# A hybrid decoder step: one more pipeline step between the root of a chunk's norm and the matrix that spreads it

## The chip, the cores and the metric

The kernel runs on one core of a Trainium2 chip. The metric is the device time of one execution in microseconds. Three executions of the kernel before took 1460.03, 1463.79 and 1465.53 us; the median is 1463.79 us.

## The reference

One layer of a decoder for 528 prompt tokens (16 learned ones and 512 given) and 64 sample tokens, with two branches side by side: a Mamba-2 state space branch and an attention branch over keys that an indexer chooses; sigmoid gates merge them, and a squared-ReLU MLP follows. The change lies in the state space branch, of which this matters:

```
# per chunk of 128 tokens, per group of 8 heads (4 groups of 512 channels)
y = einsum(cc·bc, decay, x*dt) + einsum(cc, h) * exp(acum)     # within the chunk, and from the state h
h = h * exp(last) + einsum(wj, x*dt, bc)                       # the next chunk's state
y = (y + x * d_skip) * silu(z)
y = y * rsqrt(mean(y*y over the group's 512 channels) + eps) * ssm_norm_w
```

Here tokens stand in columns and channels in partitions, so the mean over channels goes across partitions.

## The kernel before, in words

Projections, attention and MLP are matrix products in which an fp32 number is split into a rounded part and a rest (`split`, L121), so that each product is three matmuls (`mm3`, L140, issued at L145). Their weights come by DMA into a raw tile `wr`; ScalarE rounds them to `wh` (L122), VectorE makes the rest `wl` (L123).

The state space stage weaves three sources of work together. `conv_tile` and `z_tile` compute 24 + 16 tiles of the input projection (L145). `states` handles the samples' states, four units to a group. `chunk` handles one chunk of one group; there are 4 groups with 5 chunks each, in the order c = 4 (the 64 sample tokens), 0, 1, 2, 3. Each is a generator; `Pipe.push` (L91) takes in one more unit and lets every live unit run to its next `yield`, the oldest first. A group takes nine pushes: four units of `states`, then five chunks. `scan.run()` (L826) pushes on until nothing is live.

`chunk` has four steps before the change:

- the loads of `sz`, `xd`, `EB` and `bc`, the decay exponentials (L729, L731), and the product B·C with its mask (L734, L736);
- eight scaled decay tiles (L741) and their matmuls (L742), the product with the carried state (L754), the sum `y1` of both parts (L759, L760), the next state (L765 to L768), then y with skip and gate (L770, L771), its squares (L773) and their sums over the four blocks of 128 channels (L774, L775);
- a matmul with ones that sums over partitions and puts tokens in partitions (L779), and `rstd_of` (L781): mean and eps on VectorE (L154), the power -0.5 on GpSimd (L155), giving one number `ss` per token; then `rd`, a diagonal matrix with those numbers (L783, VectorE);
- a matmul of `rd` with ones that spreads the numbers over all partitions (L786, "the spread"), the scaling of `y1` by them and the norm's weight (L788, four instructions), and the write of `y1` to DRAM, `d_y` (L790). For c = 3 the final state is transposed and written too (L792 to L798).

Buffers: `y1` has three, allocated at L757 in the second step and free once the write of L790 has read it (`ho`, L796, takes one too); `ss`, `rd`, `sz`, `xd` and `EB` have two. PSUM tiles come from three tags: "w" (2 banks, projections), "a" and "s" (3 each).

What Python issues is not yet the order on an engine: the framework's scheduler places the instructions, by data dependences, free buffers and the order of issue, and so one `yield` shifts other work too. On each engine the order is then fixed. All DMAs of this stage but the gathers go through SyncE's queue, in order. The sixteen gate tiles (`gate`, L555) and the first part of the sample attention (`sample`, L849, with gathers into `Kg` and `Vg`, L860) follow, and are drawn in wherever engines have room.

Of the kernel before, what the change touches and what calls it, by code (L numbers as in the profile page):

```python
# [70 lines left out]
def body(ctx, tc, a, o):  # L71
# [42 lines left out]
    def K(n):  # L114
        s, e = CONSTS[n]
        return cst[0][:, s:e] if e <= KEPT else cst[1][:, s - KEPT:e - KEPT]
# [36 lines left out]
    def rstd_of(dst, ssq, n, cols, p=128):  # L153
        dve.tensor_scalar(dst, ssq, 1.0 / n, EPS, op0=OP.mult, op1=OP.add)  # L154
        pool.tensor_tensor(dst, dst, K("half")[:p, :cols], op=OP.pow)  # L155
# [475 lines left out]
    with tc.tile_pool(name="p3", bufs=1, reuse_waits="tile") as p3, \  # L631
# [78 lines left out]
        def chunk(g, c):  # L710
# [68 lines left out]
            pe.matmul(ps[:n, 0:1], sq[:, 0, :n], K("ones")[:, 0:1], start=True, stop=True)  # L779
            ss = p3.tile([128, 1], FT, tag="ss", name="ss", bufs=2)  # L780
            rstd_of(ss[:n], ps[:n, 0:1], 512, 1, n)  # L781
            rd = p3.tile([128, 128], FT, tag="rd", name="rd", bufs=2)
            dve.tensor_scalar(rd[:n, :n], idf[:n, :n], ss[:n], None, op0=OP.mult)  # L783
            yield
# [31 lines left out]
        for g in range(4):  # L816
            start(g)
            for j in range(9):
                scan.push(states(g, j) if j < 4 else chunk(g, (4, 0, 1, 2, 3)[j - 4]))
                next(tops, None)  # L820
                for _ in range(1 if j else 2):
                    if nxt:
                        conv.push(nxt.pop(0))
            if not nxt:
                conv.run()
# [603 lines left out]
```

## Time and profile before

| | |
|---|---|
| profiled execution, its own time | 1456.66 us |
| its span (first to last instruction) | 1454.9 us |
| median of three executions | 1463.79 us |
| TensorE (PE) matmul | 1417.8 us busy, 97% |
| VectorE (DVE) | 1096.0 us, 75% |
| ScalarE (ACT) | 755.6 us, 52% |
| GpSimd (POOL) | 328.7 us, 23% |

The chunks of the state space stage run from about 310 to 665 us of the span. Times in the rows below are in us from the span's start unless marked ns; L123 is line 123 of the kernel; "out<-in" are the program's tile names; "[x <-E t Ln]" tells how long the engine sat idle before the instruction and what ended that.

### The profile page before, as it was taken

The numbers are of one execution on the slowest core, as the hardware profiler recorded it, in microseconds if no ns is written. First come the engines' busy times: TensorE is split into PE (matmuls) and PEld (weight loads), VectorE is DVE, ScalarE is ACT, GpSimd is POOL, SyncE is SP. The second block draws the span as 40 slices with busy tenths as digits, with TensorE's granted clock in tenths as the row PEclk, the third lists the DMA queues.
The fourth block names the chain that finished last, engine by engine and source line by source line (L and its number), as shares of the span: only waits on it lengthen the run. The fifth ranks groups of instructions, "written<-read, shape, count | busy, mean of one in ns | idle before, by whom it ended". The sixth has DMA issues, their size and how long they took to land.

```text
span 1454.9 us, 26523 instructions
## 1 busy us (share of the span) xinstructions
PE 1417.8 (97%) x9808; PEld 1270.7 (87%) x9808; DVE 1096.0 (75%) x2248; ACT 755.6 (52%) x1719; POOL 328.7 (23%) x479
## 2 busy tenths in 40 slices
PE   8999999999999998999999999999999999999998
PEld 6998999988898987989688988898798988888986
DVE  6799999898769778482645777765689887888775
ACT  5553365556566655443655777832374554445441
POOL 2110011436446436251433633100000000000001
PEclk9999999999999999999999999999999999999999
DMA  7334464567676767768974532235233322322222
GB/s 204 88 76 123 126 162 126 140 194 216 181 223 184 209 185 213 222 180 260 295 240 132 154 88 85 69 104 178 80 90 100 92 89 81 88 92 86 88 70 73
DMA packets 258907, 206.73 MB, mean 142 GB/s; under 512 B 38653, under 2 KB 225905, under 8 KB 258754
## 3 DMA queue, kind: packets, MB, share of 16 engines
q1 hardware_dynamic: 253530, 186.16, 45.1%
q0 software_dynamic: 5248, 18.88, 3.9%
q8 instruction: 77, 1.26, 0.4%
q14 instruction: 52, 0.43, 0.1%
HBM read 167.83 MB, written 36.40 MB: 140 GB/s over the span
## 4 chain that ended last, share of the span: by engine, by line
PE 50%; DVE 1%; DMA 1%; issue 0%; ACT 0%; POOL 0%; POOLq 0%; DVEq 0%; ACTq 0%; SPq 0%
PE s L1184 15%; PE w L1049 7%; PE a L1309 6%; PE w L145 5%; PE w L1309 4%; PE a L145 3%; PE s L1015 2%; PE s L881 2%; PE a L1184 1%; PE a L1005 1%; PE a L904 1%; PE s L873 1%; PE s L984 1%; PE s L983 1%; PE a L894 1%; DMA jk<-h 0%
## 5 line engine op out<-in xcount | busy, mean ns | idle before, releaser
L145 PE MATMUL w<-uh,wh 128*128 128x288 f32 (+1 forms) x1168 | 359.7, 308 | 9.8 <-ACT qis L348 2.9
L145 PE MATMUL w<-ul,wh 128*128 128x288 f32 (+1 forms) x1168 | 353.5, 303 | 1.2 <-DVE ul L225 1.2
L145 PE MATMUL w<-uh,wl 128*128 128x288 f32 (+1 forms) x1168 | 354.6, 304 | 0.0
L145 PEld LDWEIGHTS w<-uh,wh 128*128 128x128 f32 x1168 | 223.9, 192 | 17.8 <-issue 4.2
L145 PEld LDWEIGHTS w<-ul,wh 128*128 128x128 f32 x1168 | 223.8, 192 | 4.4 <-issue 2.2
L145 PEld LDWEIGHTS w<-uh,wl 128*128 128x128 f32 x1168 | 222.7, 191 | 2.1 <-issue 1.7
L123 DVE TENSOR_TENSOR wl<-wr,wh 128x1024 fp32r<-128x1024 f32 x129 | 159.5, 1237 | 75.6 <-ACT wh L122 74.8
L122 ACT ACTIVATE wh<-wr 128x1024 fp32r<-128x1024 f32 x129 | 135.7, 1056 | 137.6 <-PE w L145 76.6
L1186 DVE TENSOR_TENSOR h<-h,s 128x512 f32<-128x512 f32 (+1 forms) x161 | 108.4, 680 | 57.7 <-PE s L1184 57.4
L1184 PE MATMUL s<-dh,hh 128*128 128x512 f32 (+1 forms) x302 | 118.8, 393 | 0.0
L1184 PE MATMUL s<-dl,hh 128*128 128x512 f32 (+1 forms) x302 | 118.7, 393 | 0.0
L155 POOL TENSOR_TENSOR rs<-rs,cst 128x1 f32<-128x1 f32 (+2 forms) x15 | 9.3, 619 | 415.1 <-DVE rs L154 415.0
L1184 PE MATMUL s<-dh,hl 128*128 128x512 f32 (+1 forms) x242 | 95.0, 392 | 0.0
L1049 PE MATMUL w<-ysh,wh 128*128 128x288 f32 x256 | 78.3, 308 | 0.2 <-DVE ms L1054 0.2
L122 ACT ACTIVATE dh<-wr 128x1024 fp32r<-128x1024 f32 x38 | 39.8, 1057 | 72.7 <-PE s L1184 58.5
L1049 PE MATMUL w<-ysh,wl 128*128 128x288 f32 x256 | 76.7, 300 | 0.0
L1049 PE MATMUL w<-ysl,wh 128*128 128x288 f32 x256 | 76.7, 300 | 0.0
L729 ACT ACTIVATE bc<-bc,acum 128x128 f32<-128x128 f32 (+1 forms) x160 | 49.2, 379 | 49.3 <-DMA bc<-d_ac 40.6
L594 DVE SCALAR_TENSOR_TENSOR ca<-rb,cwT,ca 128x616 f32<-128x616 f32 x72 | 68.8, 956 | 1.8 <-ACT ca L592 1.2
L1184 PEld LDWEIGHTS s<-dl,hh 128*128 128x128 f32 x302 | 56.6, 188 | 12.5
L1184 PEld LDWEIGHTS s<-dh,hh 128*128 128x128 f32 x302 | 56.7, 188 | 10.0 <-DVE h L1186 0.2
L741 DVE SCALAR_TENSOR_TENSOR bc<-bc,dts,cb 128x128 f32<-128x128 f32 (+1 forms) x160 | 57.5, 426 | 0.3
(499 smaller groups left out, 3689.9 us busy)
## 6 DMA issues: line engine op xcount, KB each, us to landing
wr<-in_w_in_dram SPq DMA_DIRECT2D x64, 512.0 KB
wr<-in_w_up_dram SPq DMA_DIRECT2D x32, 512.0 KB
wr<-in_w_down_dram SPq DMA_DIRECT2D x32, 512.0 KB
st<-in_state_ssm_dram SPq DMA_DIRECT2D x16, 512.0 KB
bc<-d_ac SPq DMA_DIRECT2D x32, 256.0 KB
out_dram<-st SPq DMA_DIRECT2D x16, 512.0 KB
wr<-in_w_ssm_proj_dram SPq DMA_DIRECT2D x16, 512.0 KB
EB<-d_ec SPq DMA_DIRECT2D x40, 128.0 KB
```

Source lines behind the costliest of these rows:

```text
L122: act.activation(hi, raw, AF.Copy)
L123: (lo_eng or dve).tensor_tensor(lo, raw, hi.bitcast(FT), op=OP.subtract)
L145: pe.matmul(ps[:, :c1 - c0], p[:, k, :], x[:, c0:c1], start=(k == 0 and i == 0), stop=(k == 7 and i == 2))
L594: dve.scalar_tensor_tensor(ca[:, 0:616], rb[:, k:k + 616], cwT[:, 24 * k + ct:24 * k + ct + 1], ca[:, 0:616], op0=OP.mult, op1=OP.add)
L729: act.activation(bc[:n, i, :n], bc[:n, i, :n], AF.Relu, scale=-1.0, bias=acum[:n, c, h0 + i:h0 + i + 1])
L741: dve.scalar_tensor_tensor(mt, mt, dts[:n, c, 8 * g + hh:8 * g + hh + 1], cb[:n, :n], op0=OP.mult, op1=OP.mult)
L881: pe.matmul(v[64 * hp:64 * hp + 64], QZ[:, hp, :], kk, start=True, stop=True)
L1015: pe.matmul(py[64 * e:64 * e + 64, 0:256], Vt[:, j, kv:kv + 64], PT[:, e, j], start=(j == 0), stop=False)
L1049: pe.matmul(ps[:, :HQ], p[:, k, mc], x[k][:, c0:c1], start=(k == 0 and i == 0), stop=(k == 3 and i == 2))
L1184: pe.matmul(ps, p, w[:, cc], start=(k == 0 and i == 0), stop=(k == len(ws) - 1 and i == len(terms) - 1))
L1186: dve.tensor_tensor(h2[:, t, cc], h2[:, t, cc], ps, op=OP.add)
L1309: pe.matmul(ps, p[:, k, :], q[:, k, :], start=(k == 0 and j == 0), stop=(k == 3 and j == 2))
```

## The change

One `yield` is put into `chunk`, after `rstd_of` and ahead of `rd`. What was the third step becomes two: the sum and the root stay at the push where they were, `rd` is issued one push later, and the spread, the scaling, the write to DRAM and (for c = 3) the final state's transposes and write one push later than before.

```
             ss = p3.tile([128, 1], FT, tag="ss", name="ss", bufs=2)
             rstd_of(ss[:n], ps[:n, 0:1], 512, 1, n)
+            yield
             rd = p3.tile([128, 128], FT, tag="rd", name="rd", bufs=2)
             dve.tensor_scalar(rd[:n, :n], idf[:n, :n], ss[:n], None, op0=OP.mult)
             yield
             rr = pst("a")
```

Lines from L782 on are one higher in the kernel after: `rd` is L784, the spread L787, the scaling L789, the write L791. No instruction is added or removed on any engine; orders differ from the second chunk on, on into the attention stages.

TensorE around chunk c = 2 of the third group, before: from that chunk's sum (L779) to its spread (L786) with what stands between (34 rows of L145 are left out).

```order
L779 MATMUL a<-cst,xd 128x1
L685 MATMUL a<-cst,st 128x128 x8
L145 MATMUL w<-uh,wh 128x288
...
L145 MATMUL w<-uh,wl 128x288
L786 MATMUL a<-rd,cst 128x128
L145 MATMUL w<-uh,wh 128x288
```

After: the first L787 here is that of the chunk before (c = 1), the second that of c = 2.

```order
L779 MATMUL a<-cst,xd 128x1
L685 MATMUL a<-cst,st 128x128 x8
...
L787 MATMUL a<-rd,cst 128x128
...
L699 MATMUL s<-Bz,xr 128x512 x3
...
L779 MATMUL a<-cst,xd 128x1
L693 MATMUL a<-sT,BC 32x128 x8
L685 MATMUL a<-cst,st 128x128 x4
...
L787 MATMUL a<-rd,cst 128x128
```

The spread of c = 2 stood 45 TensorE instructions behind its sum and stands 127 behind it now, behind the sum of c = 3.

VectorE at the end of the same group, before: `y1_6725` is c = 0's, `y1_7022` is c = 3's, which takes the same buffer, three allocations later.

```order
L788 SCALAR_TENSOR_TENSOR y1_6725<-y1_6725,nwT_84,a_6841 128x128 x4
L154 TENSOR_SCALAR ss_6850<-a_6848 128x1
...
L771 TENSOR_TENSOR y1_6877<-y1_6877,sz_6816 128x512
L788 SCALAR_TENSOR_TENSOR y1_6801<-y1_6801,nwT_84,a_6986 128x128 x4
L759 TENSOR_TENSOR y1_7022<-s_7017,EB_6894 128x512
```

After, the same two chunks are `y1_6723` and `y1_7013`.

```order
L789 SCALAR_TENSOR_TENSOR y1_6723<-y1_6723,nwT_84,a_6977 128x128 x4
L768 TENSOR_TENSOR hn_7020<-hn_7020,s_7018 128x512
L154 TENSOR_SCALAR ss_6988<-a_6986 128x1
L759 TENSOR_TENSOR y1_7013<-s_7008,EB_6885 128x512
L760 TENSOR_TENSOR y1_7013<-y1_7013,s_6991 128x512
L784 TENSOR_SCALAR rd_7051<-cst_66,ss_6988 128x128
L123 TENSOR_TENSOR wl_7901<-wr_7900,wh_7902 128x1024
```

Between the last use of the buffer by the older chunk and the first write of it by the newer stood ten rows, and stand two now; the DMA that reads the buffer has to end between them. The same pairs, of chunks c = 2 and c = 3, stand closer in the other groups too.

## Rows read from the trace of the kernel before

**Rows 1.** The page: span, busy time of PE, ACT and others.
```profile
span 1454.9 us, 26523 instructions
PE 1417.8 (97%) x9808; PEld 1270.7 (87%) x9808; DVE 1096.0 (75%) x2248; ACT 755.6 (52%) x1719; POOL 328.7 (23%) x479
```
**Rows 2.** Windows, the moved stretch: window, PE, PEld, DVE, ACT, POOL busy, clock, DMA.
```profile
290.00:700.00 410.00, 396.67 (x3048) 355.20 (x3046) 297.98 (x568) 221.84 (x537) 178.48 (x205) 0.99 0.73 207
```
**Rows 3.** Waits of PE, 290 to 700 us: total us, times, longest.
```profile
PE a L786 <- DVE rd L783: 3.1, 1, 3.1
PE w L145 <- ACT tg L283: 2.6, 2, 1.9
PE a L625 <- ACT sT L686: 2.2, 1, 2.2
...
PE s L742 <- DVE bc L741: 1.2, 3, 0.7
...
PE a L779 <- POOL xd L775: 0.8, 2, 0.4
```
**Rows 4.** Timeline of PE at the longest wait: start, duration, instruction.
```profile
575.45 0.29 PE L145 MATMUL w<-ul,wh 128*128 128x288 f32 x1
575.58 0.29 PE L145 MATMUL w<-uh,wl 128*128 128x288 f32 x1
578.93 0.49 PE L786 MATMUL a<-rd,cst 128*128 128x128 f32 x2 [3.06 <-DVE rd L783]
```
**Rows 5.** Timeline of DVE just before it.
```profile
576.96 1.92 DVE L783 TENSOR_SCALAR rd<-cst,ss 128x128 f32<-128x128 f32 x1
```
**Rows 6.** Timeline of POOL just before it.
```profile
576.45 2.34 POOL L687 TENSOR_TENSOR st<-st,elc 128x1024 f32<-128x1024 f32 x1
```
**Rows 7.** All instructions of L783: ns min/median/max, first and last start.
```profile
L783 DVE TENSOR_SCALAR rd<-cst,ss x20: 239/284/1923, 338.3 to 658.9; 128x128 f32<-128x128 f32 x16, 64x64 f32<-64x64 f32 x4
```
**Rows 8.** Windows behind two waits of PE, and one in between at full clock.
```profile
579.50:582.90 3.40, 3.40 (x18) 3.40 (x17) 2.40 (x6) 3.40 (x8) 1.33 (x1) 0.56 0.23 60
586.30:589.70 3.40, 3.40 (x37) 3.17 (x26) 0.28 (x1) 1.37 (x3) 0.55 (x1) 1.00 1.03 288
392.30:395.50 3.20, 3.20 (x14) 3.01 (x14) 2.65 (x7) 3.08 (x8) 0.25 (x2) 0.50 0.83 239
```
**Rows 9.** Timeline of SP (DMA issues), two places.
```profile
351.23 0.45 SPq L727 DMA_DIRECT2D bc<-d_ac  x1
...
663.79 0.46 SPq L790 DMA_DIRECT2D d_y<-y  x1
```
**Rows 10.** Who waited for the landing: ACT for bc, POOL for d_y.
```profile
354.08 1.06 ACT L729 ACTIVATE bc<-bc,acum 64x64 f32<-64x64 f32 x4 [0.83 <-DMA bc<-d_ac]
...
670.45 0.94 POOL L860 DMA_INDIRECT Vg<-in_cache_v_dram,idx  x1 [2.78 <-DMA d_y<-y]
```
**Rows 11.** Waits of SP's queue, 290 to 700 us.
```profile
SPq L790 <- DVE y L788: 13.2, 5, 4.8
```
**Rows 12.** Groups of DVE: busy us, mean ns of one, idle before.
```profile
L123 DVE TENSOR_TENSOR wl<-wr,wh 128x1024 fp32r<-128x1024 f32 x129 | 159.5, 1237 | 75.6 <-ACT wh L122 74.8
...
L594 DVE SCALAR_TENSOR_TENSOR ca<-rb,cwT,ca 128x616 f32<-128x616 f32 x72 | 68.8, 956 | 1.8 <-ACT ca L592 1.2
L741 DVE SCALAR_TENSOR_TENSOR bc<-bc,dts,cb 128x128 f32<-128x128 f32 (+1 forms) x160 | 57.5, 426 | 0.3
...
L768 DVE TENSOR_TENSOR hn<-hn,s 128x512 f32<-128x512 f32 x16 | 10.9, 680 | 0.9 <-PE s L765 0.8
```
**Rows 13.** Timeline of POOL: the sum of squares of c = 2, groups 1 and 2.
```profile
364.51 0.50 POOL L775 TENSOR_TENSOR xd<-xd 128x128 f32<-128x128 f32 x1
...
473.54 0.46 POOL L775 TENSOR_TENSOR xd<-xd 128x128 f32<-128x128 f32 x1
```
**Rows 14.** Timeline of PE: the matmuls that take these sums.
```profile
366.91 0.28 PE L779 MATMUL a<-cst,xd 128*128 128x1 f32 x2
...
474.05 0.38 PE L779 MATMUL a<-cst,xd 128*128 128x1 f32 x2 [0.35 <-POOL xd L775]
```

More of the change, by code (lines that the diff above doesn't have):

```diff
@@ L781, in chunk @@
             rstd_of(ss[:n], ps[:n, 0:1], 512, 1, n)
+            yield
             rd = p3.tile([128, 128], FT, tag="rd", name="rd", bufs=2)
```

## The prediction

> **What bounds the kernel now.** I read the page first: TensorE is busy for 1417.8 of the span's 1454.9 us, 97%, and VectorE, ScalarE and GpSimd have room [rows 1]. A change that adds and removes no instruction can then only win or lose time in which TensorE waits. Next the windows: in the stretch that the change rearranges most, 290 to 700 us, TensorE is busy 396.7 of 410 us, so 13.3 us are idle [rows 2]. That is all there is to win in it, but for what the clock gives back. The list of TensorE's waits says for whom: the longest single wait of the stretch is 3.1 us, for `rd`, just the instruction that the change sets back; then two waits for ScalarE with longest 1.9 and 2.2 us [rows 3]. VectorE is idle for 410 - 298.0 = 112 us of the same stretch [rows 2], and TensorE's waits for the two VectorE steps listed come to 3.1 + 1.2 = 4.3 us [rows 3]: about 4% of VectorE's idle time is felt by TensorE. Last the timeline at the longest wait: matmuls start 0.13 us apart up to 575.58 us, and the next, the spread, starts at 578.93 [rows 4].
>
> **What the change takes away.** The spread stood 45 TensorE instructions behind its chunk's sum at that place and stands 127 behind it now (the order in the section on the change). 82 instructions at 0.13 us [rows 4] are some 10.7 us of further cover, where 3.06 us were missing. The block that made `rd` late is still possible: `rd` took 1.92 us there against a median of 0.28 [rows 5, 7], while GpSimd's L687 of 2.34 us ran and ended in the same tenth of a microsecond (576.45 + 2.34 = 578.79; 576.96 + 1.92 = 578.88) [rows 5, 6]. But 1.6 us more is small against 10.7. So I count the wait as gone: -3.06 us.
>
> Behind it goes a stretch at half clock. From 579.5 to 582.9 us the granted clock is 0.56 on average, the 1.2 GHz level for nearly all of it, right after TensorE had been idle for those 3.06 us; 18 matmuls start in it, while 37 start in an equal stretch at full clock a little later [rows 8]. So 3.4 us did the work of about 1.7, and -1.7 us go with the wait. A second such stretch, with 0.50, stands at 392 us [rows 8]. Together: -4.8 us.
>
> **What it adds.** The squares, the sum and the root stay where they were; `rd`, the spread's two passes, the four scalings, one DMA issue and, for c = 3, the transposes, one copy and one more DMA are issued a push later. Their own time is unchanged. On SyncE's queue the write L790 goes behind loads that it used to precede; SP waits for the scaling at L790 in five places, 13.2 us in all [rows 11], so a later place holds up no load that was waiting before; 0. GpSimd runs nothing of the moved part. The last group's writes end a little later, and GpSimd's first `Vg` gather waits for one [rows 10]; no gather stands among TensorE's longest waits [rows 3]; 0, bounded by 2.8 us if all of that wait were felt.
>
> The real addition is a wait for a buffer. `y1` has three buffers, and each is held one push longer. So in every group the fourth and fifth chunk (c = 2 and 3), whose L759 is the first write of a buffer that was used before in that group, come soon behind the DMA that reads it: eight places. At the worst, shown in the order, two VectorE rows remain between. VectorE works in order, so what is queued behind L759 waits too: the sum L760, at that place the `rd` of the chunk before and the `wl` of a coming weight tile. I take the landing from two rows. A load of half the size was issued at 351.23 and released ScalarE by 354.08: 2.85 us [rows 9, 10]. This very write was issued at 663.79 and released GpSimd by 670.45: 6.66 us [rows 9, 10]. I take the middle, 4.7 us, from the end of the scaling, since the one row is small and the other falls in a crowd of writes. The trace of before shows no wait of this kind, so both ends are kept for the range.
>
> From 4.7 us goes what VectorE does in between. First group, c = 2: L123 and L768, 1.24 + 0.68 = 1.9 us [rows 12], wait 2.8. Second group, c = 2: L123 and two L594, and a `rd`, 1.24 + 1.91 + 0.28 = 3.4 [rows 7, 12], wait 1.3. Third group, c = 3: L768, 0.7 [rows 12], wait 4.0. In three of the other five, eight L741 and an L123 stand between, 3.4 + 1.2 = 4.6 us [rows 12]; in two an L123 and four to six others, about as much: nothing. VectorE so gets 8.1 us of new idle time, on top of 112.
>
> How much of it reaches TensorE? The wait shifts y, the squares and the sum L779, which TensorE meets in order. In the first group the sum of squares ended at 364.51 + 0.50 = 365.01 and was taken at 366.91, 1.9 us of slack [rows 13, 14], and L779 keeps its place: 2.8 - 1.9 = 0.9 us. In the second there was none (TensorE waited 0.35 us for it) [rows 13, 14], but L779 stands 7 instructions later, 0.9 us: 0.4. In the third L779 stands 12 later, 1.6 us, and I lend it the slack of the first: 4.0 - 1.9 - 1.6 = 0.5. Sum +1.8 us. At the short end (2.85 us) the waits are 0.9 and 2.2 and the slack holds them all: 0. At the long end (6.66) they are 4.7, 3.3 and 6.0, of which 2.8 + 2.4 + 2.5 = 7.7 us come through, each of them long enough to be followed by a half-clock stretch, 3 x 1.7: +12.8 us.
>
> The Trainium skill ("DMA: Bandwidth & Descriptors", Anatomy of one DMA) gives a transfer about 2.0 us fixed plus its bytes over 436 GB/s, for transfers that GpSimd issues; for these 256 KB that would be an estimate of 2.6 us, and by it no part of the new wait would reach TensorE and the time would be 1459.0 us. The load of 2.85 us fits it, the write of 6.66 us does not; the sum keeps the rows.
>
> **The sum.** -4.8 + 1.8 = -3.0 us. On the profiled execution that is 1456.66 - 3.0 = 1453.7; that execution lies 7.1 us below the median of the three that were timed, and I give the time against the median: 1463.8 - 3.0 = 1460.8 us. With both ends of the landing: 1459.0 to 1471.8.
>
> **Rivals.**
>
> The stall moves and is not removed. What made `rd` late was VectorE held beside a GpSimd instruction [rows 5, 6], and GpSimd's work is as large as before. Where the new order puts such a pair in front of L741, for which TensorE waits closely already (three times, 1.2 us) [rows 3], up to 2.3 us are lost and 1.7 of clock behind them: -4.8 + 4.0, so 1463.0 us. For it: every engine's order changes. Against it: one block in 20 `rd`s was felt. The Trainium skill ("SBUF — State Buffer", Who interferes with whom) has VectorE and GpSimd lock a shared port pair for a whole instruction, and the loser blocks; the two ends within 0.1 us of each other agree. By that rule the yield removes no block and only gives one place more cover.
>
> Slower: the third `y1` buffer decides. Price and place are the long end above: if writes in this stage land as the one at 663.79 did, 6.66 us, three waits come through, and the time is 1463.8 - 4.8 + 12.8 = 1471.8 us. It decides from a landing of about 5.5 us on, where gain and loss are near each other once the first half-clock stretch is paid. For it: the DMA engines are busy for 0.73 of this stretch [rows 2]. Against it: the half-size load of 2.85 us, and VectorE's idle time, of which 4% was felt so far.
>
> Faster: the looser coupling also clears the two ScalarE waits of 2.2 and 1.9 us [rows 3]; with a half-clock stretch behind each that is 2 x 1.7 + 4.1 = 7.5 us beside the 4.8, so 1451.5 us. For it: ScalarE's order moves too. Against it: its work is the same, and neither wait is for anything the yield moves.
>
> **How the numbers follow.** The forecast 0.55, the moved stall 0.18, the slower rival 0.13, the faster one 0.14. What a measurement of this kernel can tell from no change is about 0.5%, 7.3 us: faster below 1456.5, slower above 1471.1. Forecast and moved stall lie within it but for small tails: same 0.71, faster 0.17 (0.14 and a tail), slower 0.12. The range reaches down to the faster rival, 1451, and up past the slower one, 1473; the likeliest case's own is 1456 to 1466, which takes in the spread of the three timed runs, 5.5 us.
>
> **What would show it.** Right: no wait of the spread for `rd` among TensorE's, full clock around it; at c = 2 and 3 VectorE idle before L759, ended by the write of `y1`, some 1 to 4 us; TensorE's waits at L779 a little longer than 0.8 us in all; the same busy time. Wrong: waits of TensorE of 2 us and more behind those of L759, with more half-clock stretches than before; or the idle time of 290 to 700 us grown or shrunk by over 7 us through waits that have nothing to do with the chunk's norm.

## The result, and the profile after

The kernel after takes 1471.42 us (median of five executions, 1469.81 to 1474.28), the kernel before on the same chip 1461.16. The two medians lie 10.3 us apart; the ratio worked out from all executions is 1.0062, 95% interval 1.0044 to 1.0081: about 9 us slower, 6.4 to 11.8. That ratio is used from here on. Timed again on another chip, beside three of the experiments, it had the same ratio, 1.0062 (1.0042 to 1.0081). The prediction was 1460.8 us and no measurable change.

The page of the kernel after, whose profiled execution took 1469.81 us:

```profile
span 1468.0 us, 26503 instructions
PE 1423.6 (97%) x9808; PEld 1270.4 (87%) x9808; DVE 1099.4 (75%) x2248; ACT 753.4 (51%) x1719; POOL 321.1 (22%) x479
```

Beside [rows 1] each engine has the same count of instructions (the number behind the x), but TensorE is busy for 5.8 us longer. That is the first thing the prediction ruled out. The window that it looked at, and one behind a wait at the place of [rows 4] (columns as in [rows 2]):

```profile
290.00:700.00 410.00, 392.43 (x2993) 351.33 (x2994) 295.86 (x560) 216.17 (x528) 174.00 (x204) 0.99 0.72 205
580.10:583.50 3.40, 3.40 (x16) 3.40 (x15) 2.72 (x6) 2.01 (x5) 0.00 (x0) 0.50 0.78 197
```

TensorE's waits of 290 to 700 us (total us, times, longest), to be read against [rows 3]:

```profile
PE w L145 <- ACT tg L283: 5.3, 3, 2.2
PE a L685 <- DMA st<-in_state_ssm_dram: 3.9, 2, 3.7
PE a L685 <- DVE wl L123: 2.1, 1, 2.1
PE s L742 <- DVE bc L741: 1.7, 2, 0.8
PE w L145 <- ACT QZ L856: 1.6, 1, 1.6
```

The wait of the spread for `rd` is gone, as predicted; `rd` itself is still late at times (its longest is 1.9 us as in [rows 7], now L784):

```profile
L784 DVE TENSOR_SCALAR rd<-cst,ss x20: 239/286/1915, 340.2 to 666.4; 128x128 f32<-128x128 f32 x16, 64x64 f32<-64x64 f32 x4
```

But at the place where [rows 4] had the stall of 3.06 us, TensorE's timeline has another one, for ScalarE's L283, which empties a projection's PSUM bank:

```profile
576.54 0.29 PE L145 MATMUL w<-uh,wl 128*128 128x288 f32 x1
578.87 0.40 PE L145 MATMUL w<-uh,wh 128*128 128x288 f32 x1 [2.03 <-ACT tg L283]
```

The window at 580.1 us has granted clock 0.50, the 1.2 GHz level, and 16 matmuls in 3.40 us where 37 stood at full clock [rows 8]. So a stall and a half-clock stretch stand there in both kernels. VectorE's list of waits (whole us, times, longest) and its timeline there show the new buffer wait:

```profile
DVE y L759 <- PE s L754: 3.4, 3, 1.7
DVE y L759 <- DMA d_y<-y: 2.0, 1, 2.0
```

```profile
567.05 1.11 DVE L789 SCALAR_TENSOR_TENSOR y<-y,nwT,a 128x128 f32<-128x128 f32 x4
569.67 0.69 DVE L768 TENSOR_TENSOR hn<-hn,s 128x512 f32<-128x512 f32 x1 [1.51 <-PE s L765]
572.13 0.16 DVE L154 TENSOR_SCALAR ss<-a 128x1 f32<-128x1 f32 x1 [1.77 <-PE a L779]
574.28 0.69 DVE L759 TENSOR_TENSOR y<-s,EB 128x512 f32<-128x512 f32 x1 [2.00 <-DMA d_y<-y]
```

One listed wait, 2.0 us, at c = 3 of the third group: the place was right, the size half of the 4.0 forecast there, and the list shows no second one where 8.1 us in three were forecast. (A second profile of the same kernel lists two, 2.0 us in all, in the first and third group.) Its parts came out otherwise than in the sum, which put 4.7 us from the end of the older chunk's scaling to the landing. The scaling L789 ends at 568.16 us (567.05 + 1.11), SyncE issues the write 3.4 us later, behind seven loads, and 2.73 us after that it has landed and L759 starts: 6.1 us together. But VectorE waited 1.5 and 1.8 us for TensorE in between, which the sum left out. SyncE's issue of the write:

```profile
571.55 0.38 SPq L791 DMA_DIRECT2D d_y<-y  x1
```

**Where the time is.** The stage behind the chunks is the sample attention, woven with the output projection of the state space branch (L1049) and the prompt's attention. Its matmuls of queries and keys are L881 (L882 after), and the prompt's matmuls of attention weights and values are L1015 (L1016 after). One window from the first L881 to the last L1015 in each profile, before:

```profile
695.00:950.00 255.00, 253.52 (x1912) 211.61 (x1913) 164.49 (x515) 176.94 (x431) 94.03 (x185) 1.00 0.49 151
```

After:

```profile
701.20:963.20 262.00, 257.23 (x1914) 212.10 (x1913) 163.72 (x515) 177.58 (x432) 92.08 (x185) 1.00 0.47 144
```

The same 1912 matmul records (give or take the edges) at the same full clock take 262.0 us instead of 255.0. Of these 7.0 us, 3.7 are busy time (257.23 - 253.52) and 3.3 are waits (262.0 - 257.23 = 4.8 against 1.5). What follows had to explain both, and whether the rest of the 9 us lies in the state space stage.

**What the stage consists of.** For each of eight units b, `sample` issues six such matmuls: for pieces c0 and c1 of 512 keys and c2 of 64, each with hp = 0 and hp = 1. They are 64 columns wide (the rows show "128*64"), hp = 0 in the first half of TensorE's columns, hp = 1 in the second:

```
for hp in range(2):
    kk = KcT[:, hp, c0:c1] if c < 2 else KT[:, hp, 528:592]
    pe.matmul(v[64 * hp:64 * hp + 64], QZ[:, hp, :], kk, start=True, stop=True)
```

The keys of hp = 0 are copied by VectorE (L874), those of hp = 1 by ScalarE, and the scheduler often places the two big ones of hp = 0 first and the rest later. I call a unit joined when its six stand together, and split when full-width matmuls stand between. (A 512-wide fp32 matmul has two records in the trace.) TensorE's timeline of a joined unit, b = 2 in the kernel before:

```profile
713.79 1.94 PE L881 MATMUL s<-KcT,QZ 128*64 128x512 f32 x8
715.55 0.29 PE L881 MATMUL s<-KT,QZ 128*64 128x64 f32 x4
715.77 0.54 PE L1049 MATMUL w<-ysh,wh 128*128 128x288 f32 x2
```

And the first part of the same unit in the kernel after, where it is split:

```profile
719.10 1.90 PE L882 MATMUL s<-KcT,QZ 128*64 128x512 f32 x4
720.93 0.40 PE L1050 MATMUL w<-ysl,wh 128*128 128x288 f32 x1
```

Eight records take 1.94 us when both halves are there, four records of one half take 1.90: the halves run side by side, and a half that runs alone costs the whole time. The order on TensorE before has b = 1, 3, 5 and 7 split (and one small matmul of b = 6); after, b = 2 and b = 6 are split too, which makes six.

### The profile page after: what moved, and what is told of

The parts are those of the page before. It is cut to its first block, busy times and chain, and to the rows that moved or that the text cites. A ratio compares the mean times of both kernels' runs of the same rounds, so it can differ in the third digit from the quotient of the medians.

```text
span 1468.0 us, 26503 instructions
## 1 busy us (share of the span) xinstructions
PE 1423.6 (97%) x9808; PEld 1270.4 (87%) x9808; DVE 1099.4 (75%) x2248; ACT 753.4 (51%) x1719; POOL 321.1 (22%) x479
## 4 chain that ended last, share of the span: by engine, by line
PE 60%; DVE 6%; DMA 4%; issue 1%; ACT 1%; POOL 1%; SPq 0%; DVEq 0%; POOLq 0%; ACTq 0%
PE s L1185 15%; PE w L145 12%; PE w L1050 6%; PE a L1310 6%; PE w L1310 4%; PE a L145 3%; PE s L882 2%; PE s L1016 2%; DMA bc<-d_ac 1%; PE a L1185 1%; DMA wr<-in_w_ssm_proj_dram 1%; PE a L1006 1%; PE a L905 1%; DVE bc L741 1%; PE s L742 1%
## 5 line engine op out<-in xcount | busy, mean ns | idle before, releaser
L145 PE MATMUL w<-uh,wh 128*128 128x288 f32 (+1 forms) x1168 | 358.5, 307 | 13.6 <-ACT tg L283 5.3
L145 PE MATMUL w<-uh,wl 128*128 128x288 f32 (+1 forms) x1168 | 354.5, 303 | 0.0
L145 PE MATMUL w<-ul,wh 128*128 128x288 f32 (+1 forms) x1168 | 352.4, 302 | 1.1 <-DVE ul L225 1.1
L145 PEld LDWEIGHTS w<-uh,wh 128*128 128x128 f32 x1168 | 223.2, 191 | 22.8 <-ACT tg L283 6.0
L145 PEld LDWEIGHTS w<-ul,wh 128*128 128x128 f32 x1168 | 223.2, 191 | 3.9 <-issue 1.5
L145 PEld LDWEIGHTS w<-uh,wl 128*128 128x128 f32 x1168 | 222.1, 190 | 1.9 <-issue 1.5
L1050 PE MATMUL w<-ysh,wh 128*128 128x288 f32 x256 | 78.8, 311 | 1.1 <-DVE ms L1055 1.1
L1050 PE MATMUL w<-ysl,wh 128*128 128x288 f32 x256 | 76.8, 301 | 0.0
L1050 PE MATMUL w<-ysh,wl 128*128 128x288 f32 x256 | 76.5, 299 | 0.0
L1185 PEld LDWEIGHTS s<-dh,hh 128*128 128x128 f32 x302 | 56.7, 188 | 10.4 <-DVE h L1187 0.7
L741 DVE SCALAR_TENSOR_TENSOR bc<-bc,dts,cb 128x128 f32<-128x128 f32 (+1 forms) x160 | 57.5, 423 | 0.2
```

Of the source, the lines that this page charges most:

```text
L145: pe.matmul(ps[:, :c1 - c0], p[:, k, :], x[:, c0:c1], start=(k == 0 and i == 0), stop=(k == 7 and i == 2))
L741: dve.scalar_tensor_tensor(mt, mt, dts[:n, c, 8 * g + hh:8 * g + hh + 1], cb[:n, :n], op0=OP.mult, op1=OP.mult)
L1050: pe.matmul(ps[:, :HQ], p[:, k, mc], x[k][:, c0:c1], start=(k == 0 and i == 0), stop=(k == 3 and i == 2))
L1185: pe.matmul(ps, p, w[:, cc], start=(k == 0 and i == 0), stop=(k == len(ws) - 1 and i == len(terms) - 1))
```

## The experiments

In most of them the order on an engine is fixed: neighbours are chained by dependences that only order them and use no semaphore, from a table of instruction numbers. So the order of one kernel, or a part of it, can be given to the other. Ratios are against the kernel before on the same chip; that took 1464.2, 1462.4, 1463.9 and 1464.2 us in the four series.

**First series: which stage's order costs.**

```
     last(ORDER[-1])
+    _pin(tc)      # chains each engine's instructions in the order of a table
```

> The changed kernel with the order on every engine pinned: the slots of the state space stage's instructions (all that is issued up to the end of the chunks) in the order of the kernel after, those of the gates, the attention and all later work in the order of the kernel before. Theory 1 (the loss arises in the attention stages, whose instructions the scheduler put in another order): the state space stage gives about 3 us of loss as it does in the profile after up to 690 us, the attention nothing, so +3 us against before, about 1464. Theory 2 (the third y1 buffer and the moved steps cost it, inside the stage or by a late end of it): all of the loss is here, +10 us, about 1471.

> The converse, made from the kernel before, with no yield: the state space stage in the order of before, the gates, the attention and all later work in the order of the kernel after. Theory 1 (attention's order): +7 to +8 us against before, about 1469, although the kernel has no new step. Theory 2 (y1 and the moved steps): 0, about 1461. If the two parts interact, the two runs do not add up to the +10 us of the change.

Measured: 1473.82 us, 1.0066 (1.0047 to 1.0085), and 1491.54 us, 1.0182 (1.0162 to 1.0202). The first alone fits theory 2, the second neither. The times of both are inconclusive: weaving two orders within one stage made waits longer than those of the two kernels (4.6 us for `xd`, 4.6 for `tg`, 3.1 for `xr`). TensorE's waits of 560 to 700 us, in the first and in the second:

```profile
PE a L779 <- POOL xd L775: 8.2, 4, 4.6
```

```profile
PE w L145 <- ACT tg L283: 6.1, 2, 4.6
PE a L685 <- DMA st<-in_state_ssm_dram: 3.9, 1, 3.9
PE s L699 <- DVE xr L666: 3.1, 1, 3.1
```

The other two let the scheduler choose:

```
-            yield
+            if g < 2:        # the other kernel: if g >= 2
+                yield
```

> The new step only in groups 0 and 1 of the state space stage, the scheduler free to order the rest. Theory 2 (a price in each group for the buffer and the moved steps): about half of the loss, +5 us. Theory 1 (what the scheduler then does to the later stages, by no rule of the number of groups): anything between -5 and +15 us, and where it is far from +5 the profile has the difference behind 690 us.

> The new step only in groups 2 and 3. Theory 2: about half of the loss, +5 us, and together with the kernel that has it in groups 0 and 1 about +10. Theory 1: anything between -5 and +15 us, the two together not +10, and the difference arises behind 690 us.

Measured: 1467.26 us, 1.0018 (1.0004 to 1.0032), and 1466.90 us, 1.0015 (1.0002 to 1.0028), 2.6 and 2.2 us slower. Each is about a quarter of the loss, less than the half (4.5 us) that theory 2 wanted, and together about half of it. This speaks against a fixed price per group, though weakly, since the intervals reach to 4.7 and 4.1 us. Their profiles say more, and are read with those of the second series.

**Second series: the buffer, and the two stages cut apart.** The buffer first. The data written come from elsewhere, while the issue still waits for the scaling:

```
-            sy.dma_start(d_y[g4, :, ...], yv)
+            dw = sy.dma_start(d_y[g4, :, ...], Vt[:, 0:4, :n])
+            tc.add_manual_dep(dw.ins, sc.ins.name, ...)   # sc: the last of the four scalings
```

> The changed kernel with the order on every engine pinned to its own, and the write d_y sent from a tile that stays (Vt) instead of y1, still issued only after the scaling. So y1 comes free when the scaling ends, and no L759 waits for a DMA; every queue, order and transfer size is as before. (What is written to d_y, and so the outputs behind it, isn't the reference's.) Theory A (the third y1 buffer is what costs): the loss of 9 to 10 us goes by at least half, time 1466 or less where the kernel before takes 1461 to 1464. Theory B (the waits of L759 are 4 us on VectorE and TensorE does not feel them): within 2 us of the kernel after, about 1472.

Measured: 1471.69 us, 1.0069 (1.0049 to 1.0089), the kernel after's own ratio. In VectorE's list the wait for `d_y` is gone:

```profile
DVE y L759 <- PE s L754: 3.4, 3, 1.7
```

So the third `y1` buffer, all that the prediction charged the change with, costs nothing that these runs can tell. Theory A falls.

> The order of the kernel after on every engine up to the last matmul of the last chunk (about 688 us), and from there the order of the kernel before for all that is left; the two differ there by only 21 instructions that are already done. No order is mixed inside a stage. Theory 1 (the loss arises behind the chunks, by the order of the attention): +3 us against before, 1464 to 1467. Theory 2 (it arises inside the state space stage): +9 to +10, 1471 to 1474.

> The converse, without the new step: the order of the kernel before up to the last matmul of the last chunk, and from there that of the kernel after. Theory 1: +6 to +7 us against before, 1468 to 1471. Theory 2: 0, 1461 to 1464. If the second half only costs when it comes late (both needed), 0 here and 0 to +3 in the converse.

> The kernel after once more, beside the other three on the same chip, for its time and for a second profile: what differs between its two profiles is not the change's doing. About 1471 to 1474 if the kernel before takes 1461 to 1464. Waits for the loads of the states (st, 1.9 us in the profile of before and 3.9 in the first of after, in places where both programs are the same) should differ by some 2 us again.

Measured: 1467.74 us, 1.0033 (1.0018 to 1.0048); 1468.38 us, 1.0049 (1.0031 to 1.0067); 1470.17 us, 1.0062. In microseconds +4.8 (2.6 to 7.0) and +7.2 (4.5 to 9.8). The kernel without the new step, given only the later order, loses most of what the change loses: theory 1 holds for that part, about at its forecast (6 to 7 us). The first stays between the two theories. The last was also to show how far two profiles of one kernel differ: TensorE's waits for the states' loads (`st`) come to 5.5 us in it and 3.9 in the first. The profiles are sharper than the times, since the window from the first L881 to the last L1015 hardly varies:

| kernel | first L881 at, us | to the last L1015, us |
|---|---|---|
| before | 695.0 | 255.0 |
| first series, after's order, then before's | 712.5 | 254.6 |
| after's order, then before's | 703.0 | 255.1 |
| after | 701.2 | 262.0 |
| after again | 701.2 | 262.1 |
| after, y1 free early | 700.7 | 262.2 |
| before's order, then after's | 700.6 | 262.2 |
| first series, before's order, then after's | 723.8 | 261.8 |
| the step in groups 0 and 1 | 699.4 | 260.5 |
| the step in groups 2 and 3 | 701.2 | 261.6 |

The later order is worth 7.0 us, whatever came ahead of it. The first series fits too: what its two kernels lost besides stands ahead of the first L881. The two kernels with the step in half of the groups have later orders of their own, each with six split units, and lose 5.5 and 6.6 us in this window, nearly as much as the kernel after; why their times rose by only 2.6 and 2.2 us is open. The first column does vary: the same program up to there (before, and before's order then after's) took 695.0 and 700.6 us. The profiled execution of before, on which the prediction stood, was 5.6 us quicker to that point than the next one of the same order.

**Third series: split and joined units.** The order on TensorE alone is edited; here the b = 2 part of the first edit:

```
 L874 MATMUL s<-cst,Kg 128x128 x4
-L882 MATMUL s<-KcT,QZ_8579 64x512 x2
 L1050 MATMUL w<-ysl,wh 128x288
...
 L898 MATMUL a<-cst,P 64x128
-L882 MATMUL s<-KcT,QZ_8579 64x512 x2
+L882 MATMUL s<-KcT,QZ_8579 64x512 x4
 L882 MATMUL s<-KT,QZ_8579 64x64 x2
```

> The kernel after, its order pinned on every engine but for TensorE's matmuls of L882 in the sample units b = 2 and b = 6: there the two of the first column half (hp = 0) are set down to directly ahead of those of the second half, so that the six of the unit stand together, as they do in the kernel before. Theory H (a split unit runs its two halves one after the other instead of side by side, 1.83 to 1.86 us more): 2 x 1.6 to 1.9, so 3 to 4 us less than the kernel after, about 1467 to 1468 if that takes 1471; in the profile the two units take 1.99 us each at L882. Theory W (only TensorE's waits of the stage cost, 5.3 us there against 2.0): no change, since no wait is touched: 1471.

> The same for all seven split units (b = 1, 2, 3, 5, 6, 7 are split in the kernel after; b = 0 and 4 are not). Theory H: 1.66 + 1.69 + 1.8 + 1.85 + 2.0 + 1.8 = 10.8 us less by the times of L882 and L905 in the profile of after, less what turns into new waits: -7 to -11 us, 1460 to 1464, level with the kernel before, whose own order has four split units. Theory W: no change, 1471.

The other way round, in the kernel before (b = 2):

```
-L881 MATMUL s<-KcT,QZ_8579 64x512 x4
-L881 MATMUL s<-KT,QZ_8579 64x64 x2
+L881 MATMUL s<-KcT,QZ_8579 64x512 x2
 L1049 MATMUL w<-ysh,wh 128x288 x2
...
+L881 MATMUL s<-KcT,QZ_8579 64x512 x2
+L881 MATMUL s<-KT,QZ_8579 64x64 x2
 L904 MATMUL a<-Vg,PTs 64x128 x8
```

> The kernel before, with no new step, its order pinned but for the units b = 2 and b = 6: the four matmuls behind the first two of L881 are set down behind the next nine (b = 2) and four (b = 6) instructions of TensorE, so that full-width matmuls stand between the halves as in the kernel after. Theory H: +3 to +4 us against before; in the profile these units take 1.8 us and more twice over at L881 instead of 1.99 and 2.24 once. Theory W: no change.

> The kernel before, its order pinned but for the four units that it splits too (b = 1, 3, 5, 7) and the last matmul of b = 6: joined as above. Theory H: 1.9 + 1.6 + 2.0 + 1.7 + 0.2 = 7.4 us less by the times of L881 and L904 in the profile of before, less new waits: -4 to -7 us, so 1455 to 1458 where the kernel before takes 1462, faster than both kernels. Theory W: no change.

| kernel | time, us | ratio (interval) | first L881 to last L1015, us |
|---|---|---|---|
| after, b = 2 and 6 joined | 1470.46 | 1.0032 (1.0012 to 1.0051) | 258.1 |
| after, all joined | 1463.42 | 0.9998 (0.9981 to 1.0015) | 251.6 |
| before, b = 2 and 6 split | 1466.90 | 1.0021 (1.0008 to 1.0034) | 258.0 |
| before, all joined | 1455.63 | 0.9948 (0.9926 to 0.9970) | 247.0 |

Theory W falls in all four, in the last three by the times and in the first by the window. (The kernel after has six split units, those that the second expectation lists.) Joining the two units takes 3.9 us off the stage (forecast 3 to 4), splitting them adds 3.0 (3 to 4), joining all takes off 10.4 (10.8) and 8.0 (7.4). With the two units joined in the kernel after, TensorE's busy time in the window is 253.40 us, nearly that of the kernel before (253.52), and the idle time stays at 4.7 us. The median of the first, 1470.46, hides this: its twelve runs reach from 1462.8 to 1472.8 us, and by its ratio it lies between before and after. The windows of all joined, after and then before:

```profile
704.30:955.90 251.60, 246.33 (x1914) 209.66 (x1913) 162.91 (x515) 177.36 (x432) 92.35 (x185) 1.00 0.49 151
```

```profile
702.10:949.10 247.00, 244.84 (x1913) 209.09 (x1913) 163.44 (x515) 176.30 (x431) 94.08 (x185) 1.00 0.51 155
```

Busy time is now nearly the same (246.33 and 244.84); what is left between the orders is idle time, 5.3 against 2.2 us, the same 3 us of waits as between before and after. The list of them in the kernel after, 700 to 962 us:

```profile
PE w L1050 <- DVE ms L1055: 1.1, 2, 0.7
PE s L882 <- DVE KcT L875: 1.0, 1, 1.0
PE a L1006 <- DVE PT L1007: 0.8, 2, 0.4
PE s L874 <- DVE mxs L883: 0.6, 1, 0.6
```

And in the kernel before, 695 to 955 us:

```profile
PE s L881 <- DVE KcT L874: 1.3, 2, 0.8
PE w L145 <- ACT yah L1020: 0.5, 1, 0.5
...
PE w L1049 <- DVE ms L1054: 0.2, 1, 0.2
```

The longest in the kernel after, shown here, are small waits for VectorE, none for anything the step moved. Joining all units took away the one for `KcT` and made one of 1.3 us for ScalarE; the other three stayed.

The last of the four beats both kernels: 0.9948, 7.6 us less than the kernel before.

**Fourth series: what the predicted gain is worth by itself.** In the kernel before, the one spread that waited is moved on TensorE:

```
-L786 MATMUL a<-rd,cst 128x128
 L145 MATMUL w<-uh,wh 128x288
...
 L145 MATMUL w<-uh,wl 128x288
+L786 MATMUL a<-rd,cst 128x128
 L699 MATMUL s<-Bz,xr 128x512 x3
```

> The kernel before, its order pinned but for one instruction: the spread L786 of the third group's c = 2, the one that waits for rd, is set 27 TensorE instructions later, to just ahead of L699. It tests the largest term of the prediction by itself (-3.06 us of wait and -1.7 us of half clock). Theory G (the term is real and was taken back elsewhere in the kernel after): the wait of 3.1 to 4.1 us for rd is gone, 27 x 0.13 = 3.5 us of it hidden, but L699 behind it then waits up to 1 us for xr; -2.5 to -5 us against before, about 1459 where that takes 1463. Theory N (TensorE only waits for the next thing in the place of rd, so such a stall is worth nothing): within 1 us of before.

> Both: the spread set later, and the sample units of L881 joined (the four units that the kernel before splits). The two lie in stages apart, so the gains should add: -7.5 us of the joined units and, by theory G, -2.5 to -5, so 1451 to 1454 where the kernel before takes 1463; by theory N 1455 to 1456.

Measured: 1465.81 us, 1.0012 (0.9995 to 1.0029), and 1459.01 us, 0.9962 (0.9945 to 0.9980). The wait for `rd` is gone, and nothing is gained: theory G falls, and theory N's 1 us lies within the interval, -0.7 to 4.2 us. (The second gains a little less than the joined units alone did, 0.9948; the intervals overlap, and its window from the first L881 to the last L1015 is 248.9 us, against 247.0 there.) TensorE's timeline in the first of the two:

```profile
580.00 0.29 PE L145 MATMUL w<-uh,wl 128*128 128x288 f32 x1
583.82 0.61 PE L145 MATMUL w<-uh,wh 128*128 128x288 f32 x1 [3.53 <-ACT tg L283]
```

ScalarE's just before:

```profile
580.73 0.63 ACT L773 ACTIVATE xd<-y 128x512 f32<-128x512 f32 x1 [3.96 <-DVE y L771]
581.27 0.68 ACT L729 ACTIVATE bc<-bc,acum 128x128 f32<-128x128 f32 x2
581.85 1.03 ACT L665 CAST xr<-xb 96x1024 fp32r<-96x1024 f32 x1
582.79 0.69 ACT L729 ACTIVATE bc<-bc,acum 128x128 f32<-128x128 f32 x2
583.38 0.39 ACT L283 ACTIVATE tg<-w 128x288 f32<-128x288 f32 x1
```

And VectorE's:

```profile
577.65 3.05 DVE L771 TENSOR_TENSOR y<-y,sz 128x512 f32<-128x512 f32 x1
580.62 1.92 DVE L783 TENSOR_SCALAR rd<-cst,ss 128x128 f32<-128x128 f32 x1
```

Follow it from VectorE's product L771, which took 3.05 us. The `rd` stands behind it on VectorE, and the squares L773 wait for it on ScalarE, 3.96 us; behind the squares stands L283, which has to empty the bank for the next projection. So two things that TensorE needs are late for one reason. The spread for `rd` came first in the kernel before and hid the other. The slow product stands in the profile of the kernel before as well, right ahead of the `rd` of [rows 5]:

```profile
573.99 3.04 DVE L771 TENSOR_TENSOR y<-y,sz 128x512 f32<-128x512 f32 x1
```

In the kernel after, L283 is late at this place for another reason. It stands on ScalarE behind decay exponentials that waited 1.91 us for the load of `bc`:

```profile
576.29 1.28 ACT L729 ACTIVATE bc<-bc,acum 128x128 f32<-128x128 f32 x4 [1.91 <-DMA bc<-d_ac]
...
578.41 0.40 ACT L283 ACTIVATE tg<-w 128x288 f32<-128x288 f32 x1
```

## Why the prediction was wrong, step by step

- "A change that adds and removes no instruction can then only win or lose time in which TensorE waits." This sentence failed, and with it the choice of 290 to 700 us as all there is to look at. Half of the loss of the sample stage (3.7 of 7.0 us) is busy time: the same matmuls, fewer of them side by side. The third series shows it both ways: 3.0 us came with two splits, and 3.9 went when they were joined.
- The sum had no term for the order of the later stages, although the change's section said that orders differ on into the attention. That missing term is 7.0 of about 9 us: some 3 to 4 the two split units (shown by the third series), about 3 the waits (seen in the profiles of both orders and unchanged by joining; their cause was not tested).
- "What the change takes away", -3.06 - 1.7 us: the wait went as forecast, in every profile with the step in all four groups. The clock did not come back: 2.03 us of waiting and a stretch at 0.50 stand there again. The step read only `rd`'s own 1.92 us and not the slow product ahead of it, and the question it left out was what is late next. Moving the spread alone (1.0012) shows that in the kernel before the stall was worth nothing to TensorE, since ScalarE's L283 was late for the same cause; in the kernel after it was late for a load. The rival of the moved stall had this mechanism, but looked for it at L741.
- "What it adds", +1.8 us for the third `y1` buffer: right place, one listed wait of 2.0 us instead of 8.1 in three, and no part of it that the times can tell (1.0069 with the wait taken away, 1.0062 with it). At that place issue and landing took 6.1 us together instead of 4.7, but VectorE waited 3.3 us for TensorE meanwhile, a term that the sum did not have. The slower rival named 1471.8 us, close to the 1471.42 measured, by a mechanism that the runs rule out; that the two numbers meet is chance, and so is it that the range reaches up to the measured time.
- The base: the profiled execution of before was a quick one. In three more profiles with before's order up to the chunks' end the first L881 starts at 700.6, 701.8 and 702.1 us instead of 695.0, and the wait for `rd` is 4.0 to 4.1 us instead of 3.1, as in this list of TensorE's waits, of the kernel with before's order and then after's:

```profile
PE w L145 <- ACT tg L283: 4.6, 3, 2.6
PE a L786 <- DVE rd L783: 4.1, 1, 4.1
```

What stays open is the state space stage itself. Its end (first L881) lies at 699.9 us on the mean of the four profiles with before's order, and at 702.6 on that of the six with after's (701.2, 701.2, 700.7, 703.0, 705.0, 704.3): 2.7 us more, but executions of one order differ by up to 7. With the 7.0 us of the sample stage that makes 9.7, against 9.1 timed. Whether the step costs 0 or 4 us there these runs can't tell.

The Trainium skill has a rule that bears on the step that failed: "TensorEngine Tiling (Array Packing)", Key Properties, says that tiles of the array operate independently of each other, and that a change of the tiling drains the engine. The trace agrees with the first (eight records in 1.94 us, four of one half in 1.90) and fits the second without showing it by itself (the full-width L1050 starts at 720.93, about when the half alone is done, at 719.10 + 1.90).

## What to carry to other kernels

Where an engine works side by side within itself, as TensorE does in column halves, its busy time is no constant of the program: count what stands between the partners in the order, in every stage whose order the change moves, and not only in the stage that was edited. Before a stall is counted as a gain, look for what else is late at that moment; if two things hang on one slow instruction, removing the first wait only shows the second. And take two profiles of the kernel before, where one can: here two executions of one order differed by more than the gain that was forecast.

## What the runs showed of the hardware

The two column halves keep their own order. In unit b = 2 of the kernel after, the order on TensorE behind the split is hp = 1 of c0 and of c1, then hp = 0 and hp = 1 of c2. TensorE's timeline:

```profile
722.57 0.64 PE L882 MATMUL s<-KcT,QZ 128*64 128x512 f32 x1
722.58 0.33 PE L882 MATMUL s<-KT,QZ 128*64 128x64 f32 x2
723.05 1.02 PE L882 MATMUL s<-KcT,QZ 128*64 128x512 f32 x2
723.48 0.43 PE L905 MATMUL a<-Vg,PTs 128*64 128x128 f32 x2
```

The first of the two records of c2's small matmul (KT) starts at 722.58, 0.01 us behind c0's first, though c1 stands ahead of it in the order; and L905's first two records start at 723.48, while c1's in the other half run until after 723.90. So by these starts a half that is free goes on with its own next matmul, and does not wait for the other half's.
